# First stage of a two-layer diffusion backbone by single feature tiles, and six modulation reductions moved

## The chip, the cores and the metric

One core of a Trainium2 chip. The metric is device microseconds (us) of the launch. Engines: PE is TensorE (matmul; PEld its weight loads), DVE is VectorE, ACT is ScalarE, POOL is GpSimd, SP only issues DMAs here. Each engine works through its own instructions in order.

## The reference, cut to what matters

Two layers (0 and 1) over 512 latent tokens and 256 context tokens of width 1024, in fp32. A conditioning vector gives per-feature shifts, scales and gates ("modulation") through a weight of 1024 x 6144 per layer, once for the latent tokens (`c`) and once for the context (`c_ctx`).

```python
for l in range(DEPTH):
    sh_a, sc_a, g_a, sh_f, sc_f, g_f = jnp.split(silu_c @ mod_w[l] + mod_b[l], 6, axis=-1)
    csh_a, csc_a, cg_a, csh_f, csc_f, cg_f = jnp.split(silu_cc @ mod_w[l] + mod_b[l], 6, axis=-1)
    a_lat = modulate(h_lat, sh_a, sc_a)      # rms_norm(x) * (1 + scale) + shift
    a_ctx = modulate(h_ctx, csh_a, csc_a)
    # layer 0: latent-attention heads and neighbourhood-attention heads, one input and one output projection
    # layer 1: sliding-window grouped-query attention
    h_lat = h_lat + g_a * o_lat
    h_lat = h_lat + g_f * swiglu(modulate(h_lat, sh_f, sc_f), ffn_w_gate_up[l], ffn_w_down[l])
    ...                                      # the same for the context in layer 0
return rms_norm(h_lat, final_norm)
```

## The kernel before, in words

Activations lie feature-major: `X[k]` (k = 0 to 7) holds 128 features of 768 tokens (512 latent, then 256 context). A product of high accuracy is three matmuls on high and low parts: high by high, high by low, low by high.

*First stage (lines 804 to 960).* The latent tokens of all eight tiles are loaded, four on SP's queue and four on ACT's. ACT squares them, DVE adds, PE sums over features (L811), root and reciprocal follow (L814, L815), PE spreads the result (L351) and ACT copies it (L822) to `r`. Meanwhile PE runs `warm(n)`, n idle products of a tile of ones (L890). Shift and scale of the first norm come on PE: `chunk(comp, c)` (L839) multiplies the conditioning vector with a weight panel 256 features wide, that is two feature tiles, spread over four column groups of the array; `chunk_put` copies the sums (L845), transposes them by two small products (L846) and adds the bias (L851). `modulate` then makes the high part (L406, L407) and the low part (L408) of `A[k]`, and `start_products` (L741 to L743) multiplies it with the weights `w_start[k]` (cast and split in `load_start`, L864 and L865), the value projection of the neighbourhood heads. `latent(k)` does the four token groups of tile k, `context(k)` the two context groups. The loop runs over c = 0 to 3, two tiles at a time; the chunks of c + 1 are computed after the first tile of the pair and put after the first token group of the second. `run` fixes the order on PE, `in_turn` and `behind` fix it on DVE and ACT, and `fetch` chains the weight loads on SP.

*Then* the input projections of layer 0 (`projections`, products at L319 to L322), attention of four neighbourhood head pairs (`na_jobs`: per pair a job for the context queries and two for the latent ones) and of eight latent heads. In `attend` a job's scores (L731, L732) and softmax (L541 on DVE, L537 on ACT) are computed while the job before it is transposed (L484) and weighted (L530); side work is interleaved. The rest of an order is chosen by a list scheduler that simulates the engines.

*Later modulation.* Components 2, 4 and 3 of layer 0 are reductions on DVE: for each of the 24 feature tiles `mod_tile` loads a 128 x 1024 weight tile in two halves into `ph` and `pl` and reduces it against the latent and the context vector (L237, two halves each; L241 adds the bias). `all_mods` yields once for each vector, so 48 pairs of halves. `PACE` gives how many of these are issued in each of twelve steps of the projections (together 48), `BG` how many with each attention job (none).

## Time and profile before

| | |
|---|---|
| time, median of 3 runs (lowest to highest) | 1553.38 us (1551.88 to 1555.83) |
| the profiled execution: time, span | 1556.14 us, 1554.4 us |
| mean granted PE clock over the span | 0.995 |
| PE, DVE, ACT, POOL busy | 98%, 76%, 49%, 13% |
| moved by DMA | 225.95 MB, 145 GB/s on average |

The span runs from the first to the last instruction; the launch time is 1.74 us longer. A row of the timeline has the start, the duration, the engine, the line and the operation with the tiles it writes and reads; in brackets the idle time before it and what ended it. "x8" merges eight instructions into one row, which then lasts from the first to the last.

### The profile page before, as it was taken

The numbers are of one execution on the slowest core, as the hardware profiler recorded it, in microseconds if no ns is written. First come the engines' busy times: TensorE is split into PE (matmuls) and PEld (weight loads), VectorE is DVE, ScalarE is ACT, GpSimd is POOL, SyncE is SP. The second block draws the span as 40 slices with busy tenths as digits, with TensorE's granted clock in tenths as the row PEclk, the third lists the DMA queues.
The fourth block names the chain that finished last, engine by engine and source line by source line (L and its number), as shares of the span: only waits on it lengthen the run. The fifth ranks groups of instructions, "written<-read, shape, count | busy, mean of one in ns | idle before, by whom it ended". The sixth has DMA issues, their size and how long they took to land.

```text
span 1554.4 us, 26610 instructions
## 1 busy us (share of the span) xinstructions
PE 1524.9 (98%) x10032; PEld 1373.6 (88%) x10032; DVE 1182.5 (76%) x2420; ACT 760.7 (49%) x1523; POOL 195.4 (13%) x266
## 2 busy tenths in 40 slices
PE   9999899999999999999999999999999999999998
PEld 8788787878999898999989998877889899898997
DVE  4799987776867686867768667789867779678685
ACT  4533676673555242433424335557846455354453
POOL 0022211000111102012021122560011000000001
PEclk9999999999999999999999999999999999999999
DMA  9675654244643636547375493200224224324322
GB/s 322 245 223 182 161 143 102 57 132 135 216 136 120 232 102 219 174 146 286 117 258 183 165 341 128 68 28 1 96 81 138 82 72 137 105 76 135 89 90 88
DMA packets 80931, 225.95 MB, mean 145 GB/s; under 512 B 11233, under 2 KB 18401, under 8 KB 80801
## 3 DMA queue, kind: packets, MB, share of 16 engines
q1 hardware_dynamic: 61968, 148.73, 30.3%
q0 software_dynamic: 17680, 73.94, 13.8%
q8 instruction: 79, 1.29, 0.3%
q10 hardware_dynamic: 1152, 1.57, 0.3%
q14 instruction: 52, 0.42, 0.1%
HBM read 186.97 MB, written 23.07 MB: 135 GB/s over the span
## 4 chain that ended last, share of the span: by engine, by line
PE 75%; DVE 8%; ACT 2%; issue 2%; DMA 2%; POOL 0%; DVEq 0%; ACTq 0%; POOLq 0%
PE pss L1439 5%; PE pso L530 5%; PE pss L1438 5%; PE pss L1437 5%; PE psd L319 3%; PE psd L321 3%; PE psd L322 3%; PE pss L319 3%; PE pss L322 3%; PE pss L321 3%; PE pst L1439 3%; PE pst L1437 3%; PE pst L1438 3%; PE pst L319 2%; PE pst L321 2%; PE pst L322 2%
## 5 line engine op out<-in xcount | busy, mean ns | idle before, releaser
L308 ACT CAST wh<-wr 128x1024 fp32r<-128x1024 f32 (+2 forms) x147 | 115.1, 798 | 224.1 <-DMA wr<-in_w_dn_dram 44.6
L309 DVE TENSOR_TENSOR wl<-wr,wh 128x1024 fp32r<-128x1024 f32 (+2 forms) x144 | 130.3, 912 | 87.4 <-ACT wh L308 83.2
L537 ACT ACTIVATE p<-p,sm 128x512 f32<-128x512 f32 (+3 forms) x144 | 105.1, 731 | 30.7 <-DVE sm L541 30.1
L1437 PE MATMUL pss<-b,wh 128*128 128x384 f32 (+1 forms) x346 | 107.6, 312 | 0.5 <-ACT b L345 0.5
L1438 PE MATMUL pss<-b,wh 128*128 128x384 f32 (+1 forms) x346 | 107.8, 312 | 0.1
L1439 PE MATMUL pss<-b,wl 128*128 128x384 f32 (+1 forms) x346 | 107.1, 311 | 0.4 <-DVE wl L1425 0.4
L321 PE MATMUL psd<-b,wh 128*128 128x512 f32 (+2 forms) x254 | 88.7, 349 | 0.0
L273 DVE CUSTOM_DVE_ANT_0 p<-rope,cond 128x1024 bf16<-128x1024 f32 x64 | 76.9, 1219 | 12.3 <-DMA rope<-in_mod_w_dram 12.2
L319 PE MATMUL psd<-b,wh 128*128 128x512 f32 (+2 forms) x214 | 78.7, 368 | 0.9 <-ACT wh L308 0.3
L322 PE MATMUL psd<-b,wl 128*128 128x512 f32 (+2 forms) x214 | 77.6, 363 | 0.0
L263 POOL DMA_DIRECT2D rope<-in_mod_w_dram x48 | 25.6, 534 | 411.6 <-DVE mod L273 390.9
L530 PE MATMUL pso<-ph,b 128*64 128x256 f32 (+1 forms) x400 | 77.0, 351 | 0.4 <-DVE ph L475 0.2
L530 PE MATMUL pso<-pl,b 128*64 128x256 f32 (+1 forms) x400 | 77.2, 351 | 0.0
L1439 PE MATMUL pst<-b,wl 128*128 128x384 f32 (+1 forms) x226 | 70.7, 313 | 1.0 <-DVE wl L1425 1.0
L1437 PE MATMUL pst<-b,wh 128*128 128x384 f32 (+1 forms) x226 | 70.6, 313 | 0.6 <-ACT p L1487 0.6
L1438 PE MATMUL pst<-b,wh 128*128 128x384 f32 (+1 forms) x226 | 70.5, 312 | 0.0
L1424 ACT CAST wh<-pl 128x512 fp32r<-128x512 f32 x78 | 45.0, 619 | 51.1 <-PE pss L1438 22.5
L1424 ACT CAST wh<-wr 128x1024 fp32r<-128x1024 f32 x39 | 41.0, 1052 | 56.8 <-PE pst L1438 14.8
L319 PE MATMUL pss<-st,wh 128*128 128x512 f32 (+2 forms) x198 | 67.6, 341 | 0.3 <-ACT wh L308 0.3
L322 PE MATMUL pss<-st,wl 128*128 128x512 f32 (+2 forms) x198 | 67.6, 341 | 0.1
L321 PE MATMUL pss<-b,wh 128*128 128x256 f32 (+2 forms) x208 | 66.0, 317 | 0.0
L1437 PEld LDWEIGHTS pss<-b,wh 128*128 128x128 f32 x346 | 65.0, 188 | 1.1 <-ACT b L345 0.8
(627 smaller groups left out, 5256.8 us busy)
## 6 DMA issues: line engine op xcount, KB each, us to landing
wr<-in_w_gu_dram SPq DMA_DIRECT2D x88, 512.0 KB, 4.0
rope<-in_mod_w_dram POOLq DMA_DIRECT2D x48, 512.0 KB, 3.9
wr<-in_w_dn_dram SPq DMA_DIRECT2D x73, 256.0 KB, 2.8
wr<-in_w_out_dram SPq DMA_DIRECT2D x32, 512.0 KB, 4.0
p<-home POOLq DMA_DIRECT2D x40, 384.0 KB, 5.6
home<-p POOLq DMA_DIRECT2D x40, 384.0 KB, 5.3
wr<-in_w_in_dram SPq DMA_DIRECT2D x21, 512.0 KB, 4.0
ph<-in_mod_w_dram SPq DMA_DIRECT2D x24, 256.0 KB, 3.0
```

The lines of the kernel that those rows point to most:

```text
L273: behind(V.tensor_tensor_reduce(out=T("p", [P, D], mybir.dt.bfloat16), in0=w, in1=cond[:, v, :], op0=ALU.mult, op1=ALU.add, scale=1.0, sca ...
L308: behind(S.copy(h, r), *after[:1])
L309: behind((G if eng else V).tensor_tensor(lo, r, f(h), op=ALU.subtract), *after[1:])
L319: ins = PE.matmul(o, wh[:, k], mh[:, c], start=first and k == 0, stop=False)
L321: PE.matmul(o, wh[:, k], ml[:, c], start=False, stop=False)
L322: PE.matmul(o, wl[:, k], mh[:, c], start=False, stop=last and k == n - 1)
L530: ins = PE.matmul(o[64 * i : 64 * i + 64, c], v(kt), t, start=n == 0, stop=n == len(moving[i]) - 1)
L537: S.activation(p[:, c], p[:, c], AF.Exp, bias=nm, scale=-1.0, accum_out=dn)
L1424: S.copy(h, t)
L1437: PE.matmul(o, wh, xh, start=first and k == 0, stop=False, skip_group_check=not first)
L1438: PE.matmul(o, wh, xl, start=False, stop=False, skip_group_check=not first)
L1439: PE.matmul(o, wl, xh, start=False, stop=k == 3, skip_group_check=not first)
```

## The change

Loads and early steps: all eight token tiles are loaded by SP's queue. A small activation on `eps` at the start brings in the table of Silu before the conditioning vector arrives. `warm(44)` becomes `warm(29)`; the later ones go from 1, 2, 5 to 1, 1, 4.

The first stage goes one tile at a time. A chunk is 128 features wide (eight matmuls of 128 columns) and its weights come as two loads for a tile and component; the host lays the panels out to suit. The first tile's scale chunk and shift chunk both stand before the first transposing product, which is one per component now. `latent(k)` runs high-by-high for the four groups, then high-by-low, then low-by-high; inside it, before product n, stand the chunks and the puts of tile k + 1 (n = 4 and 8 in tile 0, n = 0 and 3 later). The context tokens are fetched two tiles at a time in k = 2 to 5, squared in k = 4 to 7, summed inside the last tile (n = 4) and spread there (n = 11), which was before the last tile's products.

The later modulation: `PACE` issues 42 pairs in the projections, `BG` one with each of the six jobs of the third and fourth neighbourhood head pair. There a weight tile is loaded and reduced in one piece of 1024 columns, in a buffer of the tag `wr`, which has three buffers.

```diff
-PACE = (3, 3, 3, 3, 5, 5, 5, 6, 5, 5, 3, 2)
+PACE = (3, 3, 3, 3, 5, 5, 5, 6, 5, 4, 0, 0)
-BG = (0, 0, 0, 0, 0)
+BG = (0, 0, 1, 1, 0)
...
+    early = S.activation(T("part", [P, 1]), eps, AF.Silu)
     for k in range(KT):
-        load = dma(X[k][:, LATS], I["xc"][k, :, LATS], (nc.sync, S)[k % 2])
-    silu.append(behind(S.activation(cond_col, cond_col, AF.Silu), load))
+        dma(X[k][:, LATS], I["xc"][k, :, LATS])
+    silu.append(behind(S.activation(cond_col, cond_col, AF.Silu), early))
...
     def mod_tile(l, comp, m, vecs):
-        for i in range(2):
-            ws.append(T(("ph", "pl")[i], [P, 512]))
+        width = 512 if dense[0] else D
+        for i in range(D // width):
+            ws.append(T(("ph", "pl")[i] if dense[0] else "wr", [P, width]))
...
+    def chunk_loads(comp, m):
+        ws = []
+        for i in range(2):
+            ws.append(T("st" if comp == 1 else ("ph", "pl")[i], [P, 512]))
+            fetch(ws[i], I["mod_wp"][PE_MODS.index((0, comp)), m // 2, 2 * (m % 2) + i])
+        return ws
+
+    def chunk(ws):
         o, ins = PM(), []
         for k in range(KT):
             g = slice(32 * (k % 4), 32 * (k % 4) + 32)
-            ins.append(PE.matmul(o[g, :NX], cond_col[:, k], w[:, NX * (k % 2) : NX * (k % 2) + NX], start=k < 4, stop=k > 3))
+            ins.append(PE.matmul(o[g, :P], cond_col[:, k], ws[k // 4][:, P * (k % 4) : P * (k % 4) + P], start=k < 4, stop=k > 3))
...
+    def latent(k, at):
+        n = 0
+        for i, (x, y) in enumerate(((0, 0), (0, 1), (1, 0))):
+            for t in range(4):
+                if n in at:
+                    at[n]()
+                ins = PE.matmul(ov[t], A[k][x][:, t * P : (t + 1) * P], starts[k][y], start=k + i == 0, stop=k == KT - 1 and i == 2)
+                run(ins, ins)
+                n += 1
...
-    warm(44)
+    warm(29)
...
+    for k in range(KT):
+        used = modulate(A[k], X[k], k, r, 0, 0, 0, LATS)
+        scaled, high = marks["scaled"], marks["high"]
+        if k == 0:
+            in_turn(s0, spread_copy, s1, parts[0], high)
+            in_turn(m0, scaled, m1, parts[1], used)
+        else:
+            in_turn(s0, s1, parts[0], high)
+            in_turn(m0, m1, scaled, parts[1], used)
+        if k in (4, 5, 6, 7):
+            for j in (2 * k - 8, 2 * k - 7):
+                acc = square_sum(acc, X[j], CTXS)
...
+        if k < KT - 1:
+            loads = [chunk_loads(comp, k + 1) for comp in (1, 0)]
+            starts.append(load_start(k + 1))
+            if k in (2, 3, 4, 5):
+                for j in (2 * k - 4, 2 * k - 3):
+                    fetch(X[j][:, CTXS], I["xc"][j, :, CTXS])
...
+            at = {4: sums, 8: puts} if k == 0 else {0: sums, 3: puts}
+        else:
...
+            at = {4: total, 11: lambda: norm_spread(context_norm[0], CTXS)}
+        latent(k, at)
```

## The prediction

> **What bounds the kernel now.** I read the page first, then windows by stage, then the timeline of the first 55 us and of 158 to 180 us, then the waits there.

> ```profile
> span 1554.4 us, 26610 instructions
> PE 1524.9 (98%) x10032; PEld 1373.6 (88%) x10032; DVE 1182.5 (76%) x2420; ACT 760.7 (49%) x1523; POOL 195.4 (13%) x266
> ```

> TensorE is the bound as a whole, but busy is not useful: the first 20 us are filled with products of a ones tile (L890), and the change touches two places that the average hides. The first is the start.

> ```profile
> 1.10 12.52 PE L890 MATMUL psd<-ones 128*128 128x128 f32 x88 [1.10 <-DVE ones L166]
> 1.20 1.86 SPq L134 DMA_DIRECT2D b<-in_xc_dram  x4
> 4.14 1.28 ACT L173 ACT_TABLE_LOAD   x1 [4.14 <-DMA cond_col<-in_cond_col_dram]
> 5.75 4.25 ACT L357 ACTIVATE p<-b 128x512 f32<-128x512 f32 x8
> 13.46 1.84 PE L811 MATMUL pst<-ones,p 128*128 128x1 f32 x16
> 15.34 0.26 ACT L814 ACTIVATE sm<-pst,eps 128x4 f32<-128x4 f32 x1 [3.85 <-PE pst L811]
> 19.81 1.45 ACT L407 ACTIVATE b<-p,mod 128x512 fp32r<-128x512 f32 x2 [0.89 <-DVE mod L851]
> 20.58 0.49 PE L741 MATMUL pss<-wh,b 128*128 128x512 f32 x1
> ```

> The squares (L357) are done at 10.0, yet the sum of squares (L811) starts at 13.46, because it stands in TensorE's order behind 44 idle products. The first real product comes at 20.58. The second place is the beginning of attention.

> ```profile
> 168.13 2.18 DVE L241 SCALAR_TENSOR_TENSOR mod<-mod,modb 128x8 f32<-128x8 f32 x1
> 171.09 0.41 DVE L541 CUSTOM_DVE_ANT_0 p<-pss,zeros 128x256 f32<-128x256 f32 x1
> 171.57 0.58 PE L731 MATMUL pss<-st,st 128*128 128x256 f32 x1 [4.23 <-DVE sm L541]
> ```
> ```profile
> 100.00:120.00 20.00, 20.00 (x112) 17.15 (x111) 19.70 (x56) 4.88 (x10) 3.61 (x7) 1.00 0.80 243
> 170.00:175.00 5.00, 3.43 (x16) 3.43 (x17) 4.12 (x15) 3.45 (x12) 0.38 (x2) 0.51 0.28 61
> ```

> (Columns of a window: length, then PE, PEld, DVE, ACT and POOL busy, granted clock, DMA share, GB/s.) VectorE is full while the input projections run (19.70 of 20) with the modulation reductions L237; its queue is late when attention starts. The first scores stand ready, the softmax step L541 comes at 171.09, TensorE idles 4.23 us, and then its clock is 0.51.

> **The change, part by part.**

> *Start.* With 29 idle products instead of 44 the queue of L890 ends near 29/44 of 12.52, at 9.4. The early activation takes the table load (1.28) out of the chain behind cond_col, so the squares may begin at about 4.6. All eight token loads now stand on SP: four take 1.86 us to issue, so the eighth goes out at 1.20 + 7 x 0.43 = 4.2.

> ```profile
> b<-in_xc_dram SPq DMA_DIRECT2D x4, 256.0 KB, 5.1
> ```

> At 5.1 us to landing the last tile is there at 9.3, its square (4.25/8, and its latency) ends at 9.9, the add on VectorE, a pass of the same size that I estimate at 0.7, at 10.6, and the second half of the sum (1.84/2) at 11.6. The square root, at 15.34 before, comes 3.7 us earlier. From there to the first product it is 5.24 us now; moving the shift chunk ahead of both transposing products and halving the chunks should save some 0.6. I take 4.3 us gained: first product at 16.3. Bounds: 3.5 (the chain behind the root unchanged) to 4.8. Two queues against one is worth nothing beyond issue time, since SP's issue stays ahead of landing.

> *Latent products, tile by tile.* The products are the same 96; what changes is how often they are interrupted.

> ```profile
> 32.45 0.59 PEld L839 LDWEIGHTS pst<-st,cond_col 128*32 128x32 f32 x16 [0.37 <-issue]
> 32.45 1.07 PE L839 MATMUL pst<-st,cond_col 128*32 128x256 f32 x16
> 33.34 0.39 PE L839 MATMUL pso<-ph,cond_col 128*32 128x256 f32 x2
> 34.32 0.50 PE L741 MATMUL pss<-wl,b 128*128 128x512 f32 x1
> 35.11 0.50 PE L846 MATMUL pst<-pick,p 128*128 128x2 f32 x4
> 35.92 0.48 PE L741 MATMUL pss<-wl,b 128*128 128x512 f32 x1
> 38.11 0.40 PE L741 MATMUL pss<-wh,b 128*128 128x512 f32 x1
> 40.67 0.39 PE L743 MATMUL pst<-wh,b 128*128 128x512 f32 x1
> 40.99 1.07 PE L839 MATMUL pst<-st,cond_col 128*32 128x256 f32 x16
> 44.29 0.50 PE L741 MATMUL pss<-wl,b 128*128 128x512 f32 x1
> ...
> 40.00:50.00 10.00, 9.91 (x68) 6.54 (x67) 7.03 (x17) 4.59 (x11) 0.00 (x0) 1.00 1.03 386
> ```

> Two tiles cost 8.54 now (32.45 to 40.99, chunk to chunk). A product costs (40.67 - 38.11)/11 = 0.233, so 24 are 5.58; the rest is a pair of chunks (32.45 to 34.32, with its entry 1.96), the two transposing steps L846 (35.11 to 35.92) and 0.2 of restarts. After the change every tile pays a pair of chunks of half width. Of the 1.96, eight steps of about 0.21 (four are 32.45 to 33.34) stream 256 columns and 0.26 is entry. If the stream halves, the pair costs 1.11; if loading the 32-column weights holds it (16 loads in 0.59 us in this profile, so 1.18 for 32), it costs 1.44. I take 1.2, nearer the stream, since weight loads overlap. Half the transposes are 0.40, restarts 0.2. So 2.79 + 1.8 = 4.59 a tile instead of 4.27, and 7 x 0.31 = 2.2 lost. Gone is the late load behind the last chunks (40.99 to 44.29 is 3.30 instead of 1.96): 1.3 won. A tile then asks for 1.31 MB in 4.59 us, or 1.57 MB in the four tiles that fetch context tokens; the chip moved 386 GB/s between 40 and 50 us, or 1.77 MB in that time. New is a wait between tiles 0 and 1: the transposes come after eight products there, and transposes, bias add, scaling (0.74), ACT (0.72) take about 2.4 us against 1.4 of cover; 1.0 lost. In the other tiles nine products (2.1) and the transposes cover it. The last tile's own sum and spread cost as much as now. So 1.9 lost by the parts; summed from the pieces the stage is 7 x 4.59 + 3.4 (the last tile with its sum and spread) + 1.0 = 36.5 against 54.34 - 20.58 = 33.8 now. The two differ by 0.8, small stops that I can't place; I take the larger loss, 2.7. Bounds: 2.1 to 4.4 by the two prices of a chunk.

> *Context start.*

> ```profile
> 51.32 0.38 PE L351 MATMUL pso<-ident_r,sm 128*128 128x128 f32 x2
> 52.67 0.51 ACT L407 ACTIVATE b<-p,mod 128x256 fp32r<-128x256 f32 x1 [0.56 <-DVE p L406]
> 54.34 0.39 PE L741 MATMUL psd<-wh,b 128*128 128x512 f32 x1
> ```

> From the spread to a ready context tile is 51.32 to 53.2, 1.9 us, now under twelve products. After the change the spread stands before the last product. TensorE has 0.4 us of cover, and the projection weights can't step in because the halves wh and wl are held by the first stage. I take 1.5 us lost (0 to 1.7; no gain, since it is covered whole now). The squares of the context ride on slack of ACT and VectorE.

> The first stage thus sums to -4.3 + 2.7 + 1.5 = -0.1: about nothing.

> *Six reductions leave the queue.*

> ```profile
> L237 DVE CUSTOM_DVE_ANT_0 p<-pl,cond,mod 128x512 bf16<-128x512 f32 x48 | 39.0, 812 | 1.4
> L237 DVE CUSTOM_DVE_ANT_0 p<-ph,cond 128x512 bf16<-128x512 f32 x48 | 36.7, 764 | 0.0
> ```

> Each is two halves, 0.81 + 0.76 = 1.58 us, six are 9.5. VectorE would be free near 161 instead of 170.3 (168.13 + 2.18), before TensorE has the first scores (8 of L731 and L732 fill the second before it stops at 167.3). The first softmax step comes at about 166.6 instead of 171.09: 4.5 won, and TensorE's idle 4.23 is gone. What is late next is VectorE's own pace. The slow clock goes with the idle time; at half speed TensorE lost about 1.7 of its 3.43 us in this window, but VectorE was busy 9.65 of the 11.40 us of that pair, so at most 1.75 can come back (0 at the least); I take 1.2.

> *The six come back in attention.* A reduction of 1024 columns in one piece is in the trace:

> ```profile
> L273 DVE CUSTOM_DVE_ANT_0 p<-rope,cond 128x1024 bf16<-128x1024 f32 x64 | 76.9, 1219 | 12.3 <-DMA rope<-in_mod_w_dram 12.2
> 171.09:182.49 11.40, 10.92 (x64) 9.56 (x64) 9.65 (x28) 9.95 (x26) 2.17 (x4) 0.75 0.75 193
> 197.31:212.60 15.29, 15.21 (x132) 12.73 (x131) 14.47 (x39) 13.05 (x35) 2.50 (x4) 1.00 0.69 176
> 230.00:243.50 13.50, 12.88 (x92) 9.36 (x92) 8.14 (x18) 8.01 (x17) 5.62 (x6) 1.00 0.47 135
> ```

> With the short read behind it I estimate 1.30. Three fall into the third head pair (197 to 212), where VectorE has 0.8 us to spare, three into the fourth, where it has 5.4 in the second half alone. Exposed is between nothing (they push side work, not the softmax) and all 3.9 of each. I take 2.6 and 0.5. Three loads of 512 KB join SP's queue; they hide while SP doesn't hold them back (a rival below).

> A half reduction of 0.81 us on average took 2.89 beside a GpSimd subtraction:

> ```profile
> 158.11 4.10 POOL L309 TENSOR_TENSOR wl<-wr,wh 128x1024 fp32r<-128x1024 f32 x2 [9.20 <-ACT wh L308]
> 158.18 2.89 DVE L237 CUSTOM_DVE_ANT_0 p<-pl,cond,mod 128x512 bf16<-128x512 f32 x1
> ```

> POOL is busy 2.50 us in the third pair, mostly with other kinds of work; one such meeting there would cost 2.1 more (2.89 - 0.81), for a sum of -0.6, and is a rival below. [...]

> Sum: -0.1 - 4.5 - 1.2 + 3.1 = -2.7. The profiled execution took 1556.14 us (span 1554.4), so 1553.4 on its own scale; the median of the three runs, 1553.38, lies 2.8 under the profiled one, and on that scale the forecast is 1550.7.

> **The rivals.** A difference under 0.3%, 4.7 us, is about what a measurement of this kernel can't tell from no change.

> *The moved reductions are hidden altogether, and the first stage gains.* If VectorE's splits for the latent heads give way to the reductions, 3.1 come back: 1547.6; with a context start that is covered, 1546.1. For it speaks the slack in the fourth pair, where those splits could go; against it that TensorE has little slack there.

> *A reduction blocks VectorE because its load stands behind a wait in SP's queue.* This is the one on the slow side.

> ```profile
> SPq L134 <- ACT b L1118: 26.8, 2, 21.4
> ```

> SP stood 21.4 us (235 to 257) on a copy that waits for ACT. The third tile is fetched in the fourth pair; if its load comes behind that copy while the reduction stands ahead of softmax steps in VectorE's order, VectorE stops. It decides once the load is later than the pair's 5 us of slack; 15 us late would cost 10: 1560.7. Against it: the copy waits for data, so an order built by time puts the load first.

> *The clock drops at the start.* The granted clock was 0.51 behind a window with 4.23 us of idling, but stayed 1.00 through this one:

> ```profile
> 347.55:350.96 3.41, 2.24 (x14) 1.57 (x14) 3.41 (x7) 2.93 (x6) 0.00 (x0) 1.00 0.22 37
> ```

> With fewer idle products I count 2.6 busy of 3.4 us between 9.6 and 13.0, so no drop. If it drops, 3.4 to 6.8 us at half speed cost 1.7 to 3.4: 1554.1 at most.

> *The moved reductions meet GpSimd.* One meeting of 2.1 us: 1552.8. For it speaks the row at 158.18; against it that POOL's 2.50 us are short pieces.

> *The stall stays.* If the order on VectorE keeps other late work ahead of the first softmax step, 5.7 of the gain is missing: 1556.4.

> **How the numbers follow.** The forecast 0.33; reductions hidden 0.34 (faster); late load 0.09 (slower); clock drop 0.06, GpSimd 0.06 and stall stays 0.08 (all three within 0.3%); all terms at their bad ends, 1559.3, 0.04 (slower). So faster 0.34, same 0.53, slower 0.13. The likeliest single case is still the forecast with the three beside it. All good ends give 1544.4, all bad ones 1559.3; the range leaves the late load and the last of each side out: 1546 to 1555.5.

> **What would show it.** Right: the first L741-type product at 16 to 17 us; tiles 4.4 to 4.9 us apart; a gap of 1 to 1.7 us before the context products; no idle TensorE and clock 1.00 at the start of attention; six reductions of 1.2 us in pairs three and four, which end later than their start allows by 2 to 4 us. Wrong: a first product after 18, tiles over 5 us, VectorE waiting for a modulation load in attention, or a clock under 1 before 20 us.

## The result and the profile after

The changed kernel takes 1569.52 us (median of four runs, 1568.87 to 1570.45) against 1554.61 us for the kernel before (1551.88 to 1556.38) on the same chip: 1.0096 times as long, 95% interval 1.0080 to 1.0112. It is slower by about 15 us, where the forecast was 2.7 us faster and the range ended at 1555.5. The profiled execution took 1568.87 us, the one of before 1556.14.

The head of the page of the changed kernel shows more span and hardly more work on any engine:

```profile
span 1567.1 us, 26816 instructions
PE 1528.5 (98%) x10126; PEld 1375.4 (88%) x10126; DVE 1177.2 (75%) x2424; ACT 761.8 (49%) x1532; POOL 195.1 (12%) x266
```

The timeline of the start (start, duration, engine, line, operation; in brackets the idle time before it and what ended it):

```profile
0.75 1.28 ACT L171 ACT_TABLE_LOAD   x1 [0.75 <-PEq L1878]
1.10 8.55 PE L900 MATMUL psd<-ones 128*128 128x128 f32 x58 [1.10 <-DVE ones L166]
10.36 2.47 PE L814 MATMUL pst<-ones,p 128*128 128x1 f32 x16 [0.70 <-DVE p L363]
12.87 0.26 ACT L817 ACTIVATE sm<-pst,eps 128x4 f32<-128x4 f32 x1 [0.83 <-PE pst L814]
14.36 1.06 PE L354 MATMUL pst<-ident_r,sm 128*128 128x128 f32 x4
19.48 1.63 PE L881 MATMUL pss<-wh,b 128*128 128x512 f32 x3
```

The table load is early, the sums (L814) start 3.1 us earlier than before and the square root (L817) comes 2.5 us earlier (3.7 forecast). But the first latent product (L881) comes at 19.48, where 20.58 stood before and 16.3 was forecast. The windows say why (length, then PE, PEld, DVE, ACT and POOL busy, granted clock, DMA share, GB/s):

```profile
8.35:11.76 3.41, 2.71 (x24) 2.52 (x22) 2.44 (x4) 3.24 (x6) 0.00 (x0) 1.00 1.07 382
11.76:15.17 3.41, 3.41 (x28) 2.83 (x27) 0.18 (x1) 0.81 (x3) 0.00 (x0) 0.50 0.99 336
18.59:22.00 3.41, 3.41 (x22) 2.54 (x25) 0.94 (x2) 0.28 (x1) 0.00 (x0) 0.50 1.05 386
22.00:25.41 3.41, 3.00 (x39) 2.46 (x32) 0.81 (x5) 1.05 (x3) 0.00 (x0) 1.00 1.04 357
```

From 11.76 to 22.00, three stretches of 3.41 us, TensorE ran at half clock. Further on, in the latent tiles and at the context products, the timeline shows two stops:

```profile
23.75 0.28 PE L854 MATMUL pst<-pick,p 128*128 128x2 f32 x2
24.44 0.35 PE L854 MATMUL pst<-pick,p 128*128 128x2 f32 x2 [0.41 <-DVE mod L859]
25.77 0.64 PE L847 MATMUL pso<-st,cond_col 128*32 128x128 f32 x16
...
61.14 0.50 PE L744 MATMUL psd<-wh,b 128*128 128x512 f32 x1 [1.29 <-ACT b L410]
```

The second transposing step of a tile waits 0.41 us for VectorE; this comes back in every one of the seven tiles. The context products wait 1.29 us for their first tile. The longest wait is in attention, in the third head pair. First SP's timeline, then VectorE's, then TensorE's, of one stretch:

```profile
195.27 9.02 SPq L134 DMA_DIRECT2D st<-st  x6
204.45 0.47 SPq L134 DMA_DIRECT2D wr<-in_mod_w_dram  x1
...
212.13 1.23 DVE L239 CUSTOM_DVE_ANT_0 p<-wr,cond 128x1024 bf16<-128x1024 f32 x1 [8.31 <-DMA wr<-in_mod_w_dram]
...
213.76 0.58 PE L734 MATMUL pss<-b,b 128*128 128x256 f32 x1 [7.51 <-DVE sm L544]
```

What SP itself waited for longest from 195 to 205 us (us, times, longest), and the window from 210 to 220 us:

```profile
SPq L134 <- DMA st<-st: 5.0, 3, 2.2
```
```profile
210.00:220.00 10.00, 6.24 (x26) 5.84 (x27) 7.87 (x19) 3.16 (x9) 0.00 (x0) 0.50 0.22 47
```

The weight tile of the first moved reduction goes out on SP's queue at 204.45, behind six copies that wait 5.0 us for earlier copies of the same kind to land, and lands at 212.1. VectorE stands 8.31 us in front of it, the softmax steps (L544) stand behind it on VectorE, and TensorE waits 7.51 us for them; its clock is at 0.50 from 209.73 to 219.97.

How late the changed kernel is against before at each milestone of the two profiled executions:

| milestone | before | after | lag |
|---|---|---|---|
| first latent product | 20.58 | 19.48 | -1.1 |
| first context product | 54.34 | 61.14 | +6.8 |
| first attention score | 166.22 | 177.24 | +11.0 |
| first MLA score (latent heads) | 242.1 | 259.3 | +17.2 |
| span | 1554.4 | 1567.1 | +12.7 |

Between context and attention the two half clocks at 62.96 and 165.36 (3.41 us each, so at most 1.7 lost each) make 3.4 of the 4.2. Some 4.5 us come back later, at most 1.7 of it because before had a half clock of 3.41 us at 958.54 that this execution lacks.

### The profile page after: what moved, and what is told of

It reads as the page before. It is cut to its first block, busy times and chain, and to the rows that moved or that the text cites. A ratio compares the mean times of both kernels' runs of the same rounds, so it can differ in the third digit from the quotient of the medians.

```text
span 1567.1 us, 26816 instructions
## 1 busy us (share of the span) xinstructions
PE 1528.5 (98%) x10126; PEld 1375.4 (88%) x10126; DVE 1177.2 (75%) x2424; ACT 761.8 (49%) x1532; POOL 195.1 (12%) x266
## 3 DMA queue, kind: packets, MB, share of 16 engines
q8 instruction: 79, 1.29, 0.3%
## 4 chain that ended last, share of the span: by engine, by line
PE 83%; DVE 9%; DMA 3%; ACT 2%; issue 2%; POOL 0%; SPq 0%; DVEq 0%; ACTq 0%; POOLq 0%
PE pss L1456 5%; PE pss L1455 5%; PE pss L1454 5%; PE pso L533 5%; PE psd L322 4%; PE psd L325 4%; PE psd L324 4%; PE pss L322 4%; PE pss L325 4%; PE pss L324 4%; PE pst L1456 3%; PE pst L1454 3%; PE pst L1455 3%; PE pst L322 3%; PE pst L324 3%; PE pst L325 3%
## 5 line engine op out<-in xcount | busy, mean ns | idle before, releaser
L276 DVE CUSTOM_DVE_ANT_0 p<-rope,cond 128x1024 bf16<-128x1024 f32 x64 | 76.9, 1220 | 11.8 <-DMA rope<-in_mod_w_dram 11.5
## 6 DMA issues: line engine op xcount, KB each, us to landing
wr<-in_w_dn_dram SPq DMA_DIRECT2D x73, 256.0 KB, 2.9
```

The lines of the kernel that those rows point to most:

```text
L276: behind(V.tensor_tensor_reduce(out=T("p", [P, D], mybir.dt.bfloat16), in0=w, in1=cond[:, v, :], op0=ALU.mult, op1=ALU.add, scale=1.0, sca ...
```

## The experiments

Every time is set against the kernel before, run beside it on the same chip (medians 1553.9 to 1554.5 in the four batches); a ratio of 0.001 is 1.55 us. The runs of one kernel differ by up to 10 us here.

**The two halves of the change.** First the new first stage with the reductions left where they were before (e1):

```diff
-PACE = (3, 3, 3, 3, 5, 5, 5, 6, 5, 4, 0, 0)
-BG = (0, 0, 1, 1, 0)
+PACE = (3, 3, 3, 3, 5, 5, 5, 6, 5, 5, 3, 2)
+BG = (0, 0, 0, 0, 0)
```

> The changed kernel with PACE and BG of the kernel before: the new first stage alone, the six reductions back in the first stage's list. Theory A (both parts of the change cost): the first stage is late by about 7 us at the first context product, the gap and the slow clock before attention stay, and the stall of 4.5 us at the start of attention is back; the late load in pair 3 and its half clock are gone. About 1555 + 7 + 4 (clock and gap) = 1560 to 1566 us, with the first attention score about 11 us or more late. Theory B (only the moved reductions cost, and the first stage's lag is made good by the time attention starts): 1552 to 1556 us.

Measured: 1558.63 us, ratio 1.0035 (1.0022 to 1.0049), so about 5 us slower. Its timeline:

```profile
1.10 9.47 PE L900 MATMUL psd<-ones 128*128 128x128 f32 x58 [1.10 <-DVE ones L166]
10.41 1.84 PE L814 MATMUL pst<-ones,p 128*128 128x1 f32 x16
16.51 0.97 PE L881 MATMUL pss<-wh,b 128*128 128x512 f32 x3 [0.17 <-ACT b L410]
```

These are the same instructions as in the changed kernel's start, but the 58 idle products end at 10.57 instead of 9.65 (their pitch falls from 0.21 to 0.11 us near 6.9 us here and near 4.9 us there, so the clock rose later), there is no gap ahead of the sums, the clock stays at 1.00, and the first product comes at 16.51. So the half clock of the changed kernel's profile is not certain at each execution. The first context product is at 57.07, 2.7 late instead of 6.8; the first score 5.4 late (a half clock of 3.4 us at 160 us among it); the wait of 4.16 us at the start of attention is back. The time lies between the two theories' ranges: the stall is back in full, as theory A has it, but the lags are less than half of what it named (7 us at the first context product, 11 at the first score).

Second, the six reductions alone, behind the old first stage (e2: PACE, BG and the 1024-wide tile of the changed kernel in the kernel before):

> The kernel before with PACE, BG and the 1024-wide reduction tile of the changed kernel: the six moved reductions alone, behind the old first stage. Theory A: the stall of 4.5 us at the start of attention goes, but the weight tile of the first reduction in pair 3 lands late and holds VectorE, and TensorE behind it, by 7 to 8 us, and a slow clock of up to 5 us follows: 1556 to 1562 us, with a wait of 7 us or more of a softmax take ahead of a score in pair 3. Theory B (the late landing comes from the shifted times of the new first stage only): the reductions are hidden and the stall is gone, 1548 to 1551 us.

Measured: 1562.82 us, ratio 1.0060 (1.0040 to 1.0080). Theory A, a little above its range. SP's, VectorE's and TensorE's timelines in the third pair:

```profile
182.81 11.10 SPq L134 DMA_DIRECT2D st<-st  x6
194.07 1.33 SPq L134 DMA_DIRECT2D wr<-in_mod_w_dram  x1
...
199.84 1.23 DVE L238 CUSTOM_DVE_ANT_0 p<-wr,cond 128x1024 bf16<-128x1024 f32 x1 [7.85 <-DMA wr<-in_mod_w_dram]
...
201.47 0.58 PE L733 MATMUL pss<-b,b 128*128 128x256 f32 x1 [7.83 <-DVE sm L543]
```

The same order, the same wait of nearly 8 us, and a half clock of some 10 us with it: the late load needs nothing of the new first stage. The ratios of the two halves, 0.0035 and 0.0060, add up to 0.0095, against 0.0096 for the whole.

**Is it SP's queue, or the DMA engines?** The changed kernel with one argument more (e3):

```diff
-            dma(ws[i], I["mod_w"][at, :, width * i : width * i + width])
+            dma(ws[i], I["mod_w"][at, :, width * i : width * i + width], None if dense[0] else G)
```

> The changed kernel with the weight tiles of the attention reductions issued by GpSimd's queue instead of SyncE's. Theory A (the tile is late because its issue stands behind six copies in SyncE's queue, 195.27 to 204.29 us): the wait of VectorE for it (8.31 us) goes, with it the half clock of 210 to 220 us: 8 to 12 us faster than the changed kernel, 1558 to 1562 us. Theory B (the DMA engines, at a share of 1.0 from 200 to 210 us, are what is late): the tile lands late all the same, 1567 to 1571 us. Theory C (the tile is early, but the copies that it displaces end later by as much): within 3 us of the changed kernel, with another wait in that place.

Measured: 1561.77 us, ratio 1.0052 (1.0034 to 1.0070), some 7 us better than the changed kernel. GpSimd's timeline:

```profile
198.10 0.53 POOL L134 DMA_DIRECT2D wr<-in_mod_w_dram  x1
```

and what VectorE waited for at the reductions' line (us, times):

```profile
its engine sat idle before it (us, times) until:
  DMA wr<-in_mod_w_dram: 0.9, 1
```

Counted from the first score (175.39 here, 177.24 in the changed kernel) the load goes out at 22.7 instead of 27.2 and the reduction starts at 29.7 instead of 34.9. The wait falls from 8.3 to 0.9 us and the half clock behind it is gone. Theory A, a little under its size; the landing itself still takes 6.9 us (7.7 before), so the crowded DMA engines (share 1.02 there) are likely the other part of the lateness; no run tests that.

**The shared bank.** In the changed kernel both transposing steps of a tile write one PSUM bank (a buffer for the results of TensorE); here each takes its own (e4):

```diff
-                d = PM()
                 for i, comp in enumerate((1, 0)):
-                    chunk_put(comp, k + 1, made[i], d[:, 2 * i : 2 * i + 2])
+                    chunk_put(comp, k + 1, made[i], PM()[:, :2])
```

> The changed kernel with the two puts of each chunk pair in two PSUM banks instead of one. Theory A (the second put waits 0.41 us in each of 7 tiles for VectorE to leave the shared bank): the pitch of the latent tiles falls from 5.0 to about 4.55 us, the first context product comes about 3 us earlier, and the kernel is 2 to 3 us faster, about 1567 us. Theory B (the pitch is set by VectorE or ScalarE, not by that wait): the pitch stays near 5.0 and the time within 1 us.

Measured: 1563.24 us, ratio 1.0052 (1.0034 to 1.0069). The timeline of a tile:

```profile
22.79 0.64 PE L847 MATMUL pst<-st,cond_col 128*32 128x128 f32 x16
24.61 0.28 PE L854 MATMUL pst<-pick,p 128*128 128x2 f32 x2
24.75 0.36 PE L854 MATMUL pso<-pick,p 128*128 128x2 f32 x2
27.25 0.64 PE L847 MATMUL pst<-st,cond_col 128*32 128x128 f32 x16
```

The wait is gone and the pitch is 4.46 us (27.25 - 22.79) instead of 5.00. From first latent to first context product it is 36.75 us (18.14 to 54.89) against 40.56 in the first stage alone: the shared bank cost 3.8 us. The wait in the trace is one for VectorE's read of the first result; whether the chip or only the program's own semaphores ask for it, the runs do not separate. The time fell by more than the 2 to 3 us expected, but the runs spread from 1556.55 to 1566.59, and the profiled one has a span only 2.3 us shorter than the changed kernel's; the size in the median I leave open. The wait for the late load is still there (TensorE's is 8.04 us).

**The start's clock.** The changed kernel with `warm(33)`, 2, 3 and 6 instead of `warm(29)`, 1, 1 and 4 (e5):

> The changed kernel with more idle products in its start: 33 instead of 29 ahead of the first sums, 2 instead of 1 ahead of the spread, 3 instead of 1 and 6 instead of 4 around the puts. Theory A (the half clock of 12.06 to 22.3 us in the changed kernel comes from its gaps and its narrow sums, and happens in most executions): the clock holds, the first latent product comes at 17 to 18 us instead of 19.48, and the kernel is 2 to 3 us faster, about 1566 us. Theory B (whether the gaps fall into one clock window is chance: the first stage alone, with the same instructions, had its first product at 16.51 us and no slow clock): the median moves by less than 1 us, since what the fill adds to the path is about what the slow clock costs on average.

Measured: 1565.74 us, ratio 1.0069 (1.0054 to 1.0084), so some 4 us better than the changed kernel; the intervals just overlap. In its timeline the first product comes at 17.14, with no half clock before 200 us. That fits theory A. The other profiles bear it out. Seven executions have the start of the changed kernel (that kernel, e1, e3, e4, and e8, e10, e11 below): three show no half clock there and have the first product at 16.51, 16.82 and 17.16; two show one of 3.41 us (17.82 and 18.14), one shows 6.83 us (18.84), and the changed kernel 10.24 us (19.48). The three with the fuller start (e5, and e14, e15 below) show none, with the first product at 17.14, 17.54 and 17.68.

**Narrow products and the clock.** The kernel before, every idle product of the start one column wide (e12):

```diff
-        ins = [PE.matmul(ov[5][:, :P], ones, ones, start=True, stop=True) for _ in range(n)]
+        ins = [PE.matmul(ov[5][:, :1], ones, ones[:, :1], start=True, stop=True) for _ in range(n)]
```

> The kernel before with each idle product of its start one column wide instead of 128 (128x1 instead of 128x128), the same number of them. Theory A (a stream of one-column products, busy as the profile shows it, does not hold TensorE's granted clock): a granted clock of 0.5 for some 7 to 10 us at the start, the first latent products at 0.43 us instead of 0.23 us each, 2 to 5 us slower. Theory B (busy is busy, whatever the width): the clock stays at 1.0 and the time changes by less than 1 us, unless the sums come earlier.

Measured: 1567.54 us, ratio 1.0089 (1.0064 to 1.0114). Its timeline:

```profile
1.10 18.94 PE L890 MATMUL psd<-ones 128*128 128x1 f32 x88 [1.10 <-DVE ones L166]
33.66 0.63 PE L742 MATMUL pss<-wh,b 128*128 128x512 f32 x1
34.09 0.63 PE L743 MATMUL pss<-wh,b 128*128 128x512 f32 x1
40.69 0.40 PE L742 MATMUL pss<-wl,b 128*128 128x512 f32 x1
40.93 0.40 PE L743 MATMUL pss<-wl,b 128*128 128x512 f32 x1
```

Theory A, and worse than I expected: TensorE shows no idle time from 1.10 on, yet it ran at half rate up to 38.5 us, the end of the first 3.41 us that held products of 512 columns alone (the 16 sums of the start, L811, last 3.55 us against 1.84 in the kernel before). The 88 one-column products take 0.215 us each where 88 wide ones took 0.142, and the first latent products follow at 0.43 us instead of 0.24. (The clock column reads 1.00 ahead of the first recorded change, here at 38.5; the pitch of the products is what tells.) In the profiles of the two kernels the half clocks that end within the span last 3.41, 6.83 or 10.24 us; here the half rate lasted through 18.94 us of one-column products, busy by the profile, and on from there to 38.5.

The same shows late in the projections. The 24 one-column sums of the latent norms come as two dozens. The recorded changes of the clock in a profile lie whole steps of 3.41 us apart (in the changed kernel's, at 11.76, 22.00, 62.96 and 66.37, they are 3, 12 and 1 steps); call such a step a window. The window of the changed kernel that holds the sums (162.42 to 165.76, 23 of the 24 start in it) and the one behind it:

```profile
161.95:165.36 3.41, 3.41 (x30) 3.31 (x29) 3.34 (x11) 1.17 (x3) 0.00 (x0) 1.00 0.00 0
165.36:168.77 3.41, 3.41 (x18) 3.41 (x18) 1.66 (x7) 1.69 (x3) 0.00 (x0) 0.50 0.00 0
```

and the two windows of the kernel before that share them, a dozen each (151.41 to 154.50):

```profile
149.58:152.99 3.41, 3.41 (x24) 3.04 (x23) 3.34 (x9) 1.88 (x2) 0.00 (x0) 1.00 0.50 154
152.99:156.41 3.42, 3.42 (x32) 3.42 (x31) 3.24 (x11) 0.79 (x3) 0.00 (x0) 1.00 0.54 153
```

TensorE is "busy" in all four. All 17 profiles divide the same way: in ten, 20 to 24 of these sums start in one window, and the next window is at half clock in all ten; in the other seven no window has more than 19, and the clock stays. No run sets where the windows fall, so this is a regularity and not an experiment. I take it for chance which case comes, as at the start, where seven profiles of the same instructions show from none to 10.24 us of half clock; that is an estimate. It is likely one reason why the runs of one kernel spread so far: in each of the 15 kernels the runs of a lower mean clock tend to be the longer ones (correlations of -0.44 to -0.94).

**Where can the six reductions go?** In the kernel before, with loads on GpSimd's queue: into attention (e6), into MLA (e7, `BG = (0, 0, 0, 0, 0.4)`), behind MLA's last softmax steps (e9, two at a time between the last steps of `attend`).

> The kernel before with the six reductions moved into attention as in the changed kernel, but with the loads of their weight tiles on GpSimd's queue. Theory A (VectorE is what attention's jobs wait for, so that 7.3 us of reductions put there cost 4 to 5 us, about what the missing stall at the start gives): 1552 to 1555 us, no change. Theory B (once the load is in time, the reductions lie beside TensorE's work, and the stall of 4.23 us with its slow clock is gone): 1547 to 1550 us.

> The kernel before with the six reductions moved past attention into the MLA stage, loads on GpSimd's queue. Theory A (in MLA VectorE is busy 75% of the time and TensorE 98 to 100%, so they are hidden there, and the stall of 4.23 us at the start of attention with its half clock goes): 1547 to 1550 us, the MLA stage as long as before, its start 4 to 6 us earlier. Theory B (the takes of MLA wait behind a reduction of 1.2 us each time, 6 of them): 1552 to 1555 us.

> The kernel before with the six reductions moved to the end of the MLA stage, behind its last takes, loads on GpSimd's queue. In the kernel before VectorE is busy 3.80 of 10 us from 356 to 366 us and 4.09 from 366 to 376 us there. Theory A (12 reductions of half a tile that leave the first stage free VectorE's backlog of 4.23 us at the start of attention, and the six whole ones cost nothing only where VectorE has idle time): MLA starts 3 to 4 us earlier as with the move into MLA, and this time the lead is kept to the end: 1549 to 1551.5 us. Theory B (a lead gained ahead of MLA is given back whatever is put there, since something else sets the start of the output products): 1553 to 1555 us.

Measured: 1557.80 us (ratio 1.0022, 1.0008 to 1.0035), 1554.97 us (1.0009, 0.9995 to 1.0024) and 1556.05 us (1.0010, 0.9997 to 1.0023). None is faster than before; e6 and e9 end above both of their theories' ranges, e7 in that of theory B. The wait of 4.23 us at the start of attention is gone in all three (one of 1.6 us for ScalarE is left, and a half clock of 3.41 us follows it, at 171.93, 170.82 and 170.48), and each place takes the gain back. In attention, what TensorE waited for softmax steps in e6 (from 167 to 244 us), and the same row of the run below that leaves the work out (e13, from 167 to 240 us):

```profile
PE pss L733 <- DVE sm L543: 2.8, 3, 1.5
```
```profile
PE pss L733 <- DVE sm L543: 0.4, 2, 0.2
```

In MLA, the window from its first score to its last in e7, 107.2 us, against 103.5 in the kernel before:

```profile
239.40:346.60 107.20, 105.72 (x784) 84.85 (x783) 83.60 (x247) 71.51 (x177) 2.47 (x4) 1.00 0.35 93
```
```profile
242.00:345.50 103.50, 103.37 (x784) 84.27 (x783) 77.34 (x233) 72.61 (x178) 1.41 (x2) 1.00 0.32 85
```

Though VectorE has some 25 us of slack there, the same number of products takes 3.7 us longer. TensorE's one long wait there, 1.3 us, is for a copy on ScalarE, and fewer than half of the products keep their place in TensorE's order, so what took the 3.7 us is not shown. At the end of MLA, waits of TensorE from 338 to 372 us in e9:

```profile
PE pst L486 <- DVE pl L477: 2.1, 1, 2.1
PE pso L532 <- DVE ph L477: 1.6, 1, 1.6
```

They are VectorE's copies out of PSUM, and they stand behind the reductions in its order. Theory A failed for both MLA moves; in e9 the trace shows why: VectorE's idle share did not hide work that stands in its order ahead of a copy that TensorE waits for. Is the lead worth anything without the work? e6 with all but 16 columns of the six reductions and their loads left out (e13):

```diff
-        width = 512 if dense[0] else D
-        for i in range(D // width):
+        width = 512 if dense[0] else 16
+        for i in range(2 if dense[0] else 1):
```

> The kernel before with the six reductions moved into attention, loads on GpSimd's queue, but over 16 of the 1024 columns only: nearly all of their work and their loads is left out. Theory A (the lead of 4 us at the start of attention is real and kept, and what took it back is the reductions' own time on VectorE): 3 to 5 us faster than the kernel before, 1549 to 1551 us. Theory B (the lead is given back by something else after attention): 1553 to 1555 us even without their work.

Measured: 1552.40 us, ratio 0.9993 (0.9984 to 1.0002). Neither theory's number: the lead is worth 1.1 us in the median (2.5 at most). In its profile MLA starts 4.8 us early and the span is 3.8 us shorter, but the profiled execution of before was itself 2 us above its median. What takes back the rest stays open. The reductions' own price in attention is the difference between this run and the one into attention: 5.4 us by the medians, 4.5 by the ratios, for 6 x 1.22 = 7.3 us of VectorE. The instructions of the softmax line (two to a step; counted by number, us after the first score) show it building up:

```
step          0      45      48      60      81
before     4.87   30.47   31.09   39.06   56.75
after      0.44   25.88   36.04   45.72   63.66
moved, GpSimd queue   0.44   27.15   32.17   40.04   58.68
moved, left out       0.44   25.88   28.29   36.92   53.57
```

Of the 5.1 us between the last two rows at number 81, 1.3 stand at number 45 already, ahead of the first reduction: the half clock at 171.93, which the last run lacks. So 3.8 us of that profile are the reductions'. The table also shows the lead itself shrinking without their work: 4.6 us at number 45, 3.2 at 81.

**Mending the new first stage.** e8 is the changed kernel with the banks apart and the reductions in MLA, e10 the same with them at the end of MLA, e11 adds an earlier context chain, e15 the fuller start to that; e14 is the first stage alone with all three.

```diff
-            if k in (2, 3, 4, 5):
-                for j in (2 * k - 4, 2 * k - 3):
+            if k in (1, 2, 3, 4):
+                for j in (2 * k - 2, 2 * k - 1):
...
-        if k in (4, 5, 6, 7):
-            for j in (2 * k - 8, 2 * k - 7):
+        if k in (3, 4, 5, 6):
+            for j in (2 * k - 6, 2 * k - 5):
...
-            at = {4: total, 11: lambda: norm_spread(context_norm[0], CTXS)}
+            at = {0: total, 6: lambda: norm_spread(context_norm[0], CTXS)}
```

> The changed kernel with the six reductions moved on into the MLA stage, their loads on GpSimd's queue, and the two puts of a chunk pair in two PSUM banks. Theory A (the first stage's lag at the first context product falls from 2.7 us, as it stood in the first stage alone, to about 0; the later stages are as in the kernel before with the reductions in MLA): 1548 to 1552 us. Theory B (the new first stage keeps its lag of about 5 us at the start of attention): 1552 to 1556 us.

> The changed kernel with the two puts in two PSUM banks and the six reductions at the end of MLA, loads on GpSimd's queue. Theory A (the new first stage, once its puts are apart, brings the first context product to where it was, but adds the gap of 1.3 us ahead of it with a half clock behind it): 0 to 2 us slower than the kernel before with the same place for the reductions, 1550 to 1553 us. Theory B (the earlier first product is worth its 3 to 4 us at the end): 1547 to 1549 us.

> As the run with the new start and the reductions at the end of MLA, but the context tokens' loads and squares one tile earlier, their sums ahead of the last tile's first product instead of its fifth, the spread ahead of its seventh instead of its twelfth. Theory A (the gap of 1.3 us at the first context product is the chain from the spread to ScalarE's modulation): the gap goes, and the half clock that follows it in four of six profiles: 2 to 3 us faster than without. Theory B (the pitch of the latent tiles is set by the loads, at 250 GB/s, and earlier context loads only push the chunks' loads back): no difference, within 1 us.

> The first stage alone (PACE and BG of the kernel before, reductions where they were), mended: puts in two banks, the context tokens' loads, squares, sums and spread earlier, and the fuller start (33, 2, 3 and 6 idle products). Theory A (bank 3.8 us, gap and its clock 1.3 to 3 us, start clock up to 3 us are all of the first stage's lag): 5 to 7 us faster than the first stage alone, 1551 to 1553 us, the first context product 2 to 4 us earlier than in the kernel before. Theory B (VectorE, with its backlog at the start of attention, takes the lead back: the stall grows by it): 1553 to 1556 us, with a wait of 6 us or more at the first takes.

> The mended first stage as in e14, with the six reductions at the end of MLA, loads on GpSimd's queue. Theory A: the start clock holds where the run without the fuller start had a half clock from 13 to 20 us; 2 to 3 us faster than that run, 1549 to 1551 us, faster than both kernels. Theory B (that half clock is chance, and the fill costs what it saves): 1551 to 1553 us.

| run | median us | ratio to before | 95% interval |
|---|---|---|---|
| e8 | 1555.76 | 1.0012 | 0.9998 to 1.0026 |
| e10 | 1556.79 | 1.0016 | 1.0002 to 1.0030 |
| e11 | 1552.17 | 0.9991 | 0.9979 to 1.0003 |
| e14 | 1553.59 | 0.9997 | 0.9987 to 1.0006 |
| e15 | 1551.31 | 0.9982 | 0.9971 to 0.9992 |

e8 against e7 and e10 against e9 are the new first stage with its bank mended against the old one: about the same. e8 falls into theory B's range; e10 lies above both of its ranges, though 0.7 us slower than e9, as its theory A has it. Bringing the context chain forward gains 4.6 us by the medians and 3.9 by the ratios (e10 to e11), more than theory A's 2 to 3; the gap of 1.3 us is gone, and the half clock at 56 us with it. In e14 the first product comes at 17.54, the first context product at 52.52 (1.8 earlier than before), the first score at 165.62 (0.6 earlier); about 1 us between the last two I did not trace. And then VectorE is not there yet:

```profile
172.15 0.58 PE L734 MATMUL pss<-st,st 128*128 128x256 f32 x1 [5.41 <-DVE sm L544]
```

The stall of before, 4.23 us, has grown by the lead and more: theory B, with a shorter wait than it named. With the reductions moved as well, e15 is the one version that beats both kernels, by 0.18% (0.08 to 0.29) against the kernel before. Its timeline shows the start at full clock and the context products without a wait of 1.3 us (no half clock before 340 us):

```profile
17.68 0.95 PE L882 MATMUL pss<-wh,b 128*128 128x512 f32 x3
52.69 0.50 PE L745 MATMUL psd<-wh,b 128*128 128x512 f32 x1
```

The fuller start by itself (e11 to e15) is not separated: the intervals overlap, and 1551.31 lies between the ranges of the two theories.

## Why the prediction was wrong

The forecast of 1550.7 us and its range failed on the slow side, through five steps. The first three belong to the moved reductions, forecast at -2.6 us and measured at about +9 alone; the last two to the first stage, forecast at -0.1 and measured at about +5 alone.

*The late load* was put at nothing in the sum and cost 5 to 8 us. It was named as a rival, "a reduction blocks VectorE because its load stands behind a wait in SP's queue", at 0.09 and 1560.7 us. The mechanism was right; the place was not. I looked for it at the wait of 21.4 us in the fourth pair and set it aside because "an order built by time puts the load first". It struck at the first of the six, in the third pair, behind six copies between tiles, and took 8.31 us of VectorE. The prediction said that the loads "hide while SP doesn't hold them back" and never looked up what SP issues in the third pair. The six reductions alone cost 9 us, and the move of the loads to another queue gave 5 to 6 of it back (1.0060 to 1.0022); behind the new first stage it gave 7 to 8.

*The value of the stall* at the start of attention, 4.5 and 1.2 in the sum, so 5.7, was nearly as far off. The stall did go: softmax instruction 45 comes 4.6 us earlier after the first score, as forecast (4.5), and the changed kernel runs at full clock from 168.77 to 209.73. But with the reductions' work left out altogether the kernel gained 1.1 us in the median (2.5 at most). Where the rest goes stays open.

*The reductions' price in attention*, 3.1 us in the sum, was 4.5 to 5.4 in the times, 3.8 of it seen in one profile. "They push side work, not the softmax" did not hold: from instruction 45 to 81 the softmax falls behind by 3.8 us.

*The clock at the start* was a rival at 0.06, "I count 2.6 busy of 3.4 us, so no drop". The count was right (2.71 in the window from 8.35 to 11.76) and the conclusion was not: the row I compared it with, 2.24 busy at clock 1.00, held products of 128 and 384 columns, and here 1.40 of the 2.71 us are one-column sums. The half clock lasted 10.24 us, not 3.4 to 6.8. It cost 3.0 us at the first product (19.48 against the 16.51 without the drop) and 4.1 at the context products (61.14 against 57.07), more than the bound of 3.4 I gave.

*The pitch of a latent tile* was mis-sized. The chunk pair costs about 1.1 us, near the 1.2 taken; "half the transposes are 0.40" is where the term failed, since both steps share a bank and the second waits for VectorE: 5.00 us a tile, not 4.59. With the bank apart it is 4.46, better than forecast. So the first stage, forecast at -0.1, was 2.7 us late at the first context product in the profile without a half clock; with the bank mended it was 0.5 late (54.89), after a half clock of 3.41 us at the start.

Right were: the start's gain without the drop (4.07 us measured in the first stage alone, 4.3 forecast) and the gap at the context products (1.29 and then 0.32, 1.5 forecast). "The moved reductions meet GpSimd" is not seen: they take 1.21 to 1.23 us each.

## What to carry to other kernels

Work moved to another place in an engine's order takes its loads with it (here the load went out behind six copies, and VectorE stood 8.31 us in front of the reduction): before moving it, read what the issuing queue does in the new place, in order, up to the first of the moved loads, and leave the load the time that the last loads there took to land. Idle share on an engine need not hide work that stands in its order ahead of a short copy which the bound engine waits for (2.1 and 1.6 us of TensorE at the end of MLA), and a stall on the bound engine can be worth less than its length (here 1.1 us for a stall of 4.2). When two small results go to one PSUM bank, look whether the second writer waits for the reader of the first, as here (0.41 us in each of seven tiles); a bank each took the wait away, and the pitch of a tile went from 5.00 to 4.46 us.
